# Queries, gates and merge gates as seven half-products per two column tiles, with attention run one pair of heads at a time from small buffers

## The chip, the cores and the metric

One core of one Trainium2 chip. The metric is device time in microseconds (us) of one execution of the whole program; lower is better.

## What is computed

One layer of a hybrid decoder for a prompt of 512 tokens and for 8 sampled sequences of 4 tokens each (32 tokens), so 544 tokens together. Everything starts from one projection with 18,952 columns; two branches follow, and a gated merge.

```python
u = einsum('btd,dc->btc', x, w_in)                # x: 544 x 2048; columns: q_m k_m v_m o_m z_m (2048 each),
                                                  # q_a 2048, k_a 256, v_a 256, z_a 2048, g_m g_a 2048 each, i, f
h_m, C, n, m = mlstm(q_m, k_m, v_m, i, f, state)  # 4 heads of 512; matrix memory C 512 x 512 per sequence and head
h_a = softmax(q_a k_a^T / 8 - slope * dist, sink) v_a   # 32 heads of 64, 4 key/value heads, window of 128 tokens
br_m = norm(h_m) * sigmoid(o_m) * silu(z_m);  br_a = h_a * silu(z_a)
y = sigmoid(g_m) * (br_m @ w_proj_m) + sigmoid(g_a) * (br_a @ w_proj_a)
out = layernorm(ALPHA * x + y @ w_out)
```

For the prompt a block of 128 queries sees its own block and the one before it. For the samples the queries see 128 cached keys and values and the new ones.

## The kernel before

All products are done in fp32r: each operand is split into a high part and the rest, and three of the four partial products are summed. The input is held in SBUF as such a split (a11, a21 for the first 8 of 16 row blocks k, two halves of 272 tokens each; the xk2 tiles for the other 8). A weight half (128 x 8 x 128) is loaded as `raw`, cast by ScalarE to `wh` (line 184), and VectorE subtracts to get `wl` (line 185); there are two buffers of each (`wp`).

**Plain product** (`gemm`, line 203): one column tile of 128 columns, 16 k x 3 partial products x 2 halves of 272 tokens = 96 matmuls (line 193).

**Pair** (`paired`, line 852): two column tiles as a 2 x 2 block product with 7 half-products instead of 8, each 8 k x 3 = 24 matmuls of 272 columns (lines 820 and 822), 168 in all. It needs sums of weight halves (VectorE, line 787), the seven splits, and sums of the results (`gather`, lines 831 to 850, ScalarE, GpSimd and VectorE) into two tiles O1 and O2 of the pool `ev`, which has three buffers. It needs sums of the input, too (s1, n2, n3 from `x_sums`, s4 from `last_sum`).

The order of the work:

1. Load and transpose the input; plain products for values (2 column tiles) and keys (2); the small gate product, and the gates' rows on VectorE beside them (`gates`, line 320). Split keys `ks` and values `VA` of all heads stay in SBUF.
2. For each of 16 pairs of heads k: a plain product for Q and one for Z; attention for pair k-1 runs beside them (`attn_heads`, line 507). Scores: 16 matmuls (line 525), each read by VectorE with a running maximum (line 527); Exp on ScalarE (line 538); scaling by VectorE (line 550); 8 transposes (line 559); the split of P (lines 218, 219); the own and the previous block are cut out by GpSimd products with the 0/1 masks `own_` and `prev_` (lines 564, 566); 16 matmuls of P times V (line 573); two sums (line 577) and the product with silu(z) (line 582).
3. Plain products for the first 10 of 32 merge-gate tiles; beside seven of them the sample attention (`sample_attention`, line 666) and the input sums.
4. 51 pairs: per mLSTM head six for v, k, q and four for o, z (`end_oz`, line 1071), then 11 for the other merge gates. Beside them the sample heads of the mLSTM (`sample_head`, line 1007): each loads, updates and stores 8 memories C of 1 MB from two buffers.
5. Plain products with w_proj_a beside the prompt's mLSTM; then w_proj_m; then w_out with the layer norm.

Work "beside" a product is a Python generator: `spawn` puts it on a list, and `tick` lets each take one step (to its next `yield`). `paired` calls `tick` after half-products 1, 3, 5 and 6, four times in a pair. This fixes the order in which instructions are traced; a list scheduler then places them on the engines at compile time, by that order, by dependences and by free buffers. Each engine's instructions run in the placed order. All DMAs are issued from the SP queue, in order.

Of the kernel before, what the change touches and what calls it, by code (L numbers as in the profile page):

```python
# [21 lines left out]
SEQ = 512  # L22
# [51 lines left out]
def _build(tc, nc, i, o, es):  # L74
# [59 lines left out]
    cc = cst.tile([128, C_N], F32, name="cc")  # L134
# [17 lines left out]
    esP = ExitStack()  # L152
    sp = pool(esP, "sp", 1)
    gas = sp.tile([128, 16, NS], F32, name="gas")
    qas = sp.tile([128, 2, NB, GRP, NTS], F32, name="qas")
    kas = sp.tile([128, 2, NS], F32, name="kas")
    vas = sp.tile([32, 256], F32, name="vas")

    d_brm = dr.tile([16, 128, T], F32, name="d_brm")
    d_bra = dr.tile([16, 128, T], F32, name="d_bra")  # L160
    d_q = dr.tile([16, 128, T], F32, name="d_q")
# [84 lines left out]
    esB = ExitStack()  # L246
    b1 = pool(esB, "b1", 1)
    bk = pool(esB, "bk", 4)
    esG = ExitStack()
    t544 = pool(esG, "t544", 17)  # L250
# [32 lines left out]
    nc.sync.dma_start(cc[:, 128:C_N], i["consts"][:, 128:C_N])  # L283
# [147 lines left out]


    VA = b1.tile([128, 4, KVH, 128], F32R, name="VA")
    kbp = b1.tile([128, 256], F32, name="kbp")
    vbp = b1.tile([128, 256], F32, name="vbp")
    kns = b1.tile([32, 256], F32, name="kns")
    own_ = b1.tile([128, 128], F32, name="own_")
    prev_ = b1.tile([128, 128], F32, name="prev_")
    V.tensor_scalar(own_[:], cc[:, C_TRI:C_TRI + 128], -1.0, None, op0=ALU.is_ge)
    V.tensor_scalar(prev_[:], own_[:], -1.0, 1.0, op0=ALU.mult, op1=ALU.add)  # L440
    ks = {}

    def attn_values(kk, vt):
        pt = sm()
        for b in range(4):
            PE.transpose(pt[:, b * 128:b * 128 + 128], vt[:, b * 128:b * 128 + 128], ident)
        pt2 = sm()
        PE.transpose(pt2[:32, 0:128], vt[:, SEQ:T], ident)
        src = pt[:].rearrange("p (b k d) -> p b k d", b=4, k=2)
        hilo(src, VA[:, :, 2 * kk:2 * kk + 2, 0:64], VA[:, :, 2 * kk:2 * kk + 2, 64:128])  # L450
        V.tensor_copy(vbp[:, kk * 128:kk * 128 + 128], pt[:, 384:512])
        V.tensor_copy(vas[:, kk * 128:kk * 128 + 128], pt2[:32, 0:128])
        if kk == 1:
            nc.sync.dma_start(vb_p[0].rearrange("t k d -> t (k d)"), vbp[:])
            for b in range(NB):
                nc.sync.dma_start(vb_s[b, 124:128].rearrange("t k d -> t (k d)"), vas[b * NTS:b * NTS + NTS])

    def attn_keys(kk, kt):
        for a in range(2):
            k1 = bk.tile([128, SEQ], F32R, tag="k1", name=nm("k1"))  # L460
            k2 = bk.tile([128, SEQ], F32R, tag="k2", name=nm("k2"))
            own, oth = slice(a * 64, a * 64 + 64), slice(64 - a * 64, 128 - a * 64)
            V.tensor_copy(k1[own], kt[own, 0:SEQ])
            A.copy(k1[oth], kt[own, 0:SEQ])
            V.tensor_tensor(out=k2[own], in0=kt[own, 0:SEQ], in1=r32(k1[own]), op=ALU.subtract)
            V.tensor_tensor(out=k2[oth], in0=kt[own, 0:SEQ], in1=r32(k1[own]), op=ALU.subtract)
            ks[2 * kk + a] = (k1, k2)
        yield
# [3 lines left out]
        V.tensor_copy(kbp[:, kk * 128:kk * 128 + 128], pt[:, 0:128])  # L472
        V.tensor_copy(kns[:, kk * 128:kk * 128 + 128], pt[:32, 128:256])
        if kk == 1:
            nc.sync.dma_start(kb_p[0].rearrange("t k d -> t (k d)"), kbp[:])
            for b in range(NB):
                nc.sync.dma_start(kb_s[b, 124:128].rearrange("t k d -> t (k d)"), kns[b * NTS:b * NTS + NTS])

    for kk in range(2):
        ps = gemm(win, VA_ + kk * 128, xh, xl, raws=((raw0[0], raw0[1]), (raw0[2], None))[kk])  # L480
        if kk == 0:
            spawn(gates(gates_product()))
        vt = ev()
        A.copy(two(vt[:]), pv(ps))
        attn_values(kk, vt)
    for kk in range(2):
        ps = gemm(win, KA + kk * 128, xh, xl)
        kt = ev()
        A.copy(two(kt[:]), pv(ps))
        V.tensor_copy(kas[:, kk], kt[:, SEQ:T])  # L490
        g_ = attn_keys(kk, kt)
        next(g_)
        spawn(g_)
    drain()
    esG.close()
    esB2 = ExitStack()
    b2 = pool(esB2, "b2", 2)
    bq = pool(esB2, "bq", 6)
    bs = pool(esB2, "bs", 6)
    bP = pool(esB2, "bP", 2)  # L500
    bt = pool(esB2, "bt", 1)
    bz = pool(esB2, "bz", 2)
    bm = pool(esB2, "bm", 4)
    nc.sync.dma_start(kb_s[:, 0:124], i["state_attn_k"][:, NTS:128])
    nc.sync.dma_start(vb_s[:, 0:124], i["state_attn_v"][:, NTS:128])

    def attn_heads(k, qs, hT):

        kvh = k // 4
        k1, k2 = ks[kvh]  # L510
        nb = b2.tile([128, 2, 256], F32, tag="nb", name=nm("nb"))
        for a in range(2):
            G.tensor_scalar(nb[:, a], cc[:, C_DIST:C_DIST + 256], -SLOPES[2 * k + a], None, op0=ALU.mult)
        sums = bm.tile([128, 4, 2], F32, tag="sums", name=nm("sums"))
        mx = bm.tile([128, 4, 2], F32, tag="mx", name=nm("mx"))
        mn = bm.tile([128, 4, 2], F32, tag="mn", name=nm("mn"))
        S = []
        for j in range(4):
            w0 = 128 if j == 0 else 0
            k0 = max(j - 1, 0) * 128  # L520
            pp = sm()
            s_ = bs.tile([128, 2, 256], F32, tag="s", name=nm("s"))
            for a in range(2):
                for n, kx in enumerate((k1, k2)):
                    PE.matmul(pp[:, a * 256 + w0:a * 256 + 256], qs[a][:, j * 128:j * 128 + 128],  # L525
                              kx[:, k0:k0 + 256 - w0], start=(n == 0), stop=(n == 1))
                V.tensor_tensor_reduce(s_[:, a, w0:256], pp[:, a * 256 + w0:a * 256 + 256], nb[:, a, w0:256], 1.0,  # L527
                                       sinkb[:, 2 * k + a:2 * k + a + 1], ALU.add, ALU.max,
                                       accum_out=mx[:, j, a:a + 1])
            S.append(s_)  # L530
            if j == 1:
                yield
        V.tensor_scalar(mn[:], mx[:], -1.0, None, op0=ALU.mult)
        for j in range(4):
            w0 = 128 if j == 0 else 0
            for a in range(2):
                s_ = S[j][:, a, w0:256]
                A.activation(s_, s_, AF.Exp, bias=mn[:, j, a:a + 1], accum_out=sums[:, j, a:a + 1])
# [15 lines left out]
        for a in range(2):  # L554
# [23 lines left out]
            if a == 0:  # L578
                yield
# [939 lines left out]
```

## Time and profile before

| | |
|---|---|
| three runs, median (lowest, highest) | 2608.9 us (2605.08, 2615.58) |
| the profiled execution's own time | 2608.22 us |
| its span | 2606.4 us |
| granted TensorE clock, mean | 0.996 of full |
| stage 1 (to the first Q product) | about 0 to 90 us |
| stage 2 (attention) | about 90 to 577 us |
| stage 3 (gate tiles, sample attention) | about 577 to 688 us |
| stage 4 (pairs) | 688 to 1870 us |
| stage 5 | 1870 to 2606 us |

How to read the profile: PE is TensorE (PEld its weight loads, which overlap the matmuls), DVE is VectorE, ACT ScalarE, POOL GpSimd, SP the queue that issues DMAs. "L193" is line 193 of the kernel. A row of a group gives the line, the engine, the operation, output <- inputs, the shape, how often (x), busy us and mean ns, then the engine's idle time just before these instructions and what ended it. In the chain of waits each row is a stretch of the chain that ended last: start, duration, what ran. Matmul durations are latencies of a pipeline: what one costs is the distance from one start to the next.

### The profile page before, as it was taken

Reading aid. Unit: us, or ns where it says so; the run is one execution under the profiler, and the core shown is the slowest. Engines: PE = TensorE matmul, PEld = TensorE weight load, DVE = VectorE, ACT = ScalarE, POOL = GpSimd, SP = SyncE. Lnnn points to the kernel's source line nnn. Section 1 sums busy time; section 2 is a strip of 40 time slices with the busy share of each in tenths; the row PEclk is TensorE's granted clock in tenths of the full one; section 3 lists DMA queues with packets and bytes.
Section 4 is the critical chain, followed back from the end, with each engine's and each line's share of the span. In section 5 each row is a group of like instructions: output and inputs, shape, how many; then the busy total and the mean of one; then the engine's idle time right before and its main releaser. Section 6 shows DMA issues by size and latency. Waiting matters only on the chain.

```text
span 2606.4 us, 48797 instructions
## 1 busy us (share of the span) xinstructions
PE 2572.9 (99%) x20378; PEld 2508.7 (96%) x20378; DVE 1657.6 (64%) x2428; ACT 1013.1 (39%) x1562; POOL 479.7 (18%) x467
## 2 busy tenths in 40 slices
PE   8999999999999999999999999999999999999997
PEld 8999999999999999999999999999999999999997
DVE  5666656646667877787787778777766553333336
ACT  3345545544334433433443343444633332222221
POOL 0245554541001220122122112200000000000002
PEclk9999999999999999999999999999999999999999
DMA  6322233243444575377447745764555455445432
GB/s 184 84 82 82 82 94 82 74 139 91 132 128 117 178 232 177 108 226 243 132 134 232 216 113 172 246 188 123 177 177 171 159 163 165 132 140 178 115 93 90
DMA packets 513229, 381.33 MB, mean 146 GB/s; under 512 B 30912, under 2 KB 435216, under 8 KB 512720
## 3 DMA queue, kind: packets, MB, share of 16 engines
q1 hardware_dynamic: 513008, 378.21, 48.5%
q8 instruction: 160, 2.62, 0.4%
q14 instruction: 61, 0.50, 0.1%
HBM read 295.43 MB, written 84.75 MB: 146 GB/s over the span
## 4 chain that ended last, share of the span: by engine, by line
PE 89%; DMA 6%; DVE 3%; issue 1%; ACT 1%; POOL 0%; SPq 0%; DVEq 0%; ACTq 0%; POOLq 0%
PE mm L193 41%; PE mm L820 24%; PE mm L822 11%; DMA C<-in_state_mlstm_C 3%; PE sm L1185 2%; DMA out<-C 2%; PE sm L1217 1%; PE sm L525 1%; PE sm L1030 1%; PE sm L1230 1%; PE sm L573 1%; ACT wh L184 1%; DVE wl L185 1%; PE sm L193 1%; PE sm L1034 1%
## 5 line engine op out<-in xcount | busy, mean ns | idle before, releaser
L184 ACT CAST wh<-raw 128x1024 fp32r<-128x1024 f32 x541 | 567.3, 1049 | 1123.3 <-PE mm L820 563.5
L185 DVE TENSOR_TENSOR wl<-raw,wh 128x1024 fp32r<-128x1024 f32 x541 | 702.0, 1305 | 348.6 <-ACT wh L184 345.7
L787 DVE TENSOR_TENSOR raw<-raw,raw 128x1024 f32<-128x1024 f32 x204 | 255.1, 1250 | 2.9 <-DMA raw<-in_w_in 0.2
L193 PE MATMUL mm<-xk,wh 128*128 128x272 f32 x1472 | 248.7, 290 | 0.0
L820 PE MATMUL mm<-xk,wh 128*128 128x272 f32 x1632 | 222.4, 288 | 1.1 <-ACT ev L839 1.1
L820 PEld LDWEIGHTS mm<-xk,wh 128*128 128x128 f32 x1632 | 211.8, 188 | 7.2 <-issue 3.4
L193 PE MATMUL mm<-bh,wl 128*128 128x272 f32 x1024 | 214.0, 289 | 0.0
L193 PE MATMUL mm<-bh,wh 128*128 128x272 f32 x1024 | 213.7, 290 | 0.0
L193 PE MATMUL mm<-bl,wh 128*128 128x272 f32 x1024 | 213.3, 288 | 0.0
L193 PEld LDWEIGHTS mm<-xk,wh 128*128 128x128 f32 x1472 | 208.4, 189 | 0.2
L840 POOL TENSOR_TENSOR ev<-p,ev 128x272 f32<-128x272 f32 x51 | 72.2, 1416 | 563.7 <-ACT ev L839 563.7
L193 PEld LDWEIGHTS mm<-bh,wh 128*128 128x128 f32 x1024 | 160.7, 188 | 2.3 <-issue 2.3
L193 PEld LDWEIGHTS mm<-bl,wh 128*128 128x128 f32 x1024 | 161.4, 188 | 0.0
L193 PEld LDWEIGHTS mm<-bh,wl 128*128 128x128 f32 x1024 | 160.8, 189 | 0.0
L193 PE MATMUL mm<-xk,wl 128*128 128x272 f32 x736 | 153.1, 289 | 0.0
L527 DVE CUSTOM_DVE_ANT_0 s<-sm,nb,sinkb 128x256 f32<-128x256 f32 (+1 forms) x128 | 57.2, 449 | 117.4 <-PE sm L525 117.3
L822 PE MATMUL mm<-xk,wl 128*128 128x272 f32 x816 | 118.4, 287 | 0.0
L193 PEld LDWEIGHTS mm<-xk,wl 128*128 128x128 f32 x736 | 115.8, 189 | 0.0
L820 PE MATMUL mm<-n2h,wh 128*128 128x272 f32 x408 | 107.2, 295 | 3.5 <-ACT wh L184 3.5
L193 PE MATMUL mm<-a11h,wl 128*128 128x272 f32 x368 | 108.4, 294 | 0.0
L193 PE MATMUL mm<-a11l,wh 128*128 128x272 f32 x368 | 108.3, 294 | 0.0
L822 PEld LDWEIGHTS mm<-xk,wl 128*128 128x128 f32 x816 | 108.3, 188 | 0.0
(436 smaller groups left out, 6255.1 us busy)
## 6 DMA issues: line engine op xcount, KB each, us to landing
raw<-in_w_in SPq DMA_DIRECT2D x296, 512.0 KB
C<-in_state_mlstm_C SPq DMA_DIRECT2D x32, 1024.0 KB
out<-C SPq DMA_DIRECT2D x64, 512.0 KB
raw<-in_w_proj_a SPq DMA_DIRECT2D x32, 512.0 KB
raw<-in_w_proj_m SPq DMA_DIRECT2D x32, 512.0 KB
raw<-in_w_out SPq DMA_DIRECT2D x32, 512.0 KB
d_sga<-ev SPq DMA_DIRECT2D x16, 272.0 KB
d_sgm<-ev SPq DMA_DIRECT2D x16, 272.0 KB
```

The source lines that it names most:

```text
L184: A.copy(wh[:], raw[:])
L185: V.tensor_tensor(out=wl[:], in0=raw[:], in1=r32(wh[:]), op=ALU.subtract)
L193: PE.matmul(ps[:, f, :w], a[:, kk], b(k, c, w), start=(k == 0 and n == 0), stop=(k == 15 and n == 2))
L525: PE.matmul(pp[:, a * 256 + w0:a * 256 + 256], qs[a][:, j * 128:j * 128 + 128], kx[:, k0:k0 + 256 - w0], start=(n == 0), stop=(n == 1))
L527: V.tensor_tensor_reduce(s_[:, a, w0:256], pp[:, a * 256 + w0:a * 256 + 256], nb[:, a, w0:256], 1.0, sinkb[:, 2 * k + a:2 * k + a + 1], AL ...
L573: PE.matmul(po[:, b * 128:b * 128 + n], VA[:, b, kvh], P_[:, 2 * b:2 * b + n // 128], start=(b == 0 and m == 0), stop=(b == 3 and m == 1), ...
L787: V.tensor_tensor(out=w[out][:], in0=w[a][:], in1=w[b][:], op=ALU.add)
L820: PE.matmul(ps, wh[:, k], x(p, k), start=(first and k == 0 and p == 0), stop=False, skip_group_check=True)
L822: PE.matmul(ps, wl[:, k], x(0, k), start=False, stop=(k == 7), skip_group_check=True)
L840: G.tensor_tensor(out=c22, in0=p1, in1=c11, op=ALU.subtract)
L1030: PE.matmul(pC[c * 32:c * 32 + 32, :], qz[:, c], ct[:, c], start=(b == 0), stop=(b == NB - 1), tile_position=(0, c * 32))
L1185: PE.matmul(pp[:, 0:258], a[:, b * 128:b * 128 + 128], b_[:, b, f], start=(b == 0 and n == 0), stop=(b == 3 and n == 2))
```

## The change

Q and Z of a pair of heads k become one pair (Q tile, Z tile), and each merge gate pair is (GA tile, GM tile); no gate tile is a plain product any more. There are 72 pairs: 16 for Q and Z, 40 for the mLSTM, 16 for the merge gates. Only values and keys are plain products.

To have room for the input sums during attention, attention's buffers shrink: the split keys and values of one key/value head at a time (written to DRAM as they are computed, read back and split again every fourth pair of heads), scores tiles for one pair of heads, one sz, one hT. Values are used with their differences: `DV[j] = V[j] - V[j-1]`, so that P times V is `V[j-1] P + DV[j] (own P)`; only the product with `own_` is left on GpSimd, and P times V has 14 matmuls of 128 columns per head instead of 8 (6 of 256 columns, 2 of 128). The alibi table `nb` is scaled by ScalarE. The sample columns of q, z, k, v go to DRAM and are read back by the sample attention, which runs when all heads are done. Only then are the pools of the mLSTM's sample heads opened, in the memory that attention and sample attention held; `end_oz` asks for this. `tick` is called after half-products 0, 1, 3, 4 and 6. The core of the diff:

```diff
+    s1, n2, n3 = quad(act2, "s1"), quad(act2, "n2"), quad(act2, "n3")
...
-    t544 = pool(esG, "t544", 17)
+    t544 = pool(esG, "t544", 12)
+    tx = pool(esG, "tx", 4)
...
+        nc.sync.dma_start(d_vr[0:SEQ, cs].rearrange("(b p) c -> p b c", p=128), blk(vr[:]))
...
+        nc.sync.dma_start(d_ka[kk], kt[:])
...
-    for kk in range(2):
-        ps = gemm(win, VA_ + kk * 128, xh, xl, raws=((raw0[0], raw0[1]), (raw0[2], None))[kk])
-        if kk == 0:
-            spawn(gates(gates_product()))
...
+    for kk in range(2):
+        ps = gemm(win, VA_ + kk * 128, xh, xl, raws=((raw0[0], raw0[1]), (raw0[2], None))[kk], every=4)
+        if kk == 0:
+            spawn(x_sums())
+            gates_ps = gates_product()
...
-            if n % 2 or n == 6:
+            if n in (0, 1, 3, 4, 6):
                 tick()
...
+    def open_attention():
+        for name, bufs in (("b1", 1), ("bs", 2), ("bt", 1), ("bq", 2), ("bm", 2)):
+            bp[name] = pool(esB, name, bufs)
...
+    def kv_head(kvh):
+        kk, r = kvh // 2, (kvh % 2) * 64
+        raw = scores_tile()
...
+        for half in (0, 64):
+            nc.sync.dma_start(kraw[half:half + 64], d_ka[kk, r:r + 64, 0:SEQ])
+        nc.sync.dma_start(vraw, d_vr[0:SEQ, kvh * 64:kvh * 64 + 64].rearrange("(b p) c -> p b c", p=128))
...
+        hilo(kraw, k1[:], k2[:])
+        hilo(vraw, VA[:, :, 0:64], VA[:, :, 64:128])
+        V.tensor_tensor(out=dv[:, 1:4], in0=vraw[:, 1:4], in1=vraw[:, 0:3], op=ALU.subtract)
+        hilo(dv[:, 1:4], DV[:, 1:4, 0:64], DV[:, 1:4, 64:128])
...
+    def attention(k, qs, sz, kv):
...
+        for a in range(2):
+            nb = btile("b1", [128, 256], f"nb{a}")
+            A.activation(nb[:], cc[:, C_DIST:C_DIST + 256], AF.Copy, scale=-SLOPES[2 * k + a])
...
+            st.append((s_, mx, mn, sums, sink))
+            yield
...
+            for o_, p_ in ((oh, ph), (ol, pl)):
+                G.tensor_tensor(out=o_[:], in0=r32(p_[:]), in1=own_[:].unsqueeze(1).to_broadcast([128, 4, 128]),
+                                op=ALU.mult)
+            yield
...
+            for j in range(4):
+                o_ = slice(j * 128, j * 128 + 128)
+                if j:
+                    todo += [(o_, VA[:, j - 1], p_[:, j]) for p_ in (ph, pl)]
+                todo += [(o_, DV[:, j] if j else VA[:, 0], p_[:, j]) for p_ in (oh, ol)]
+            for n, (o_, v_, p_) in enumerate(todo):
+                PE.matmul(po[:, o_], v_, p_, start=(n == 0), stop=(n == len(todo) - 1), skip_group_check=True)
...
+    def end_qz(k):
+        def end(o1, o2):
+            until(lambda: state["open"] and state["done"] == k)
...
+            nc.sync.dma_start(d_qa[k], o1[:, SEQ:T])
+            sz = btile("b1", [128, T], "sz")
+            A.activation(sz[:], o2[:], AF.Sigmoid)
+            V.tensor_tensor(out=sz[:], in0=o2[:], in1=sz[:], op=ALU.mult)
+            nc.sync.dma_start(d_bra[k][:, SEQ:T], sz[:, SEQ:T])
+            waiting[k] = (qs, sz)
...
+    def attentions():
+        while gates_ in live:
+            yield
+        for _ in last:
+            pass
+        esG.close()
+        open_attention()
+        state["open"] = True
+        for k in range(16):
+            if k % 4 == 0:
+                kv = kv_head(k // 4)
+            while k not in waiting:
+                yield
+            yield from attention(k, *waiting.pop(k), kv)
+            state["done"] = k + 1
+        esB.close()
+        yield from sample_attention()
+        esT.close()
+        open_samples()
+        state["samples"] = True
...
     def end_oz(k):
         def end(o, z_):
-            sg = pz.tile([128, T], F32, tag="sz", name=nm("sz"))
+            until(lambda: state["samples"])
+            sg = st1([128, T], "sz", p="pz")
...
+    fill = merge_gates[:8] + [w for h in range(3) for w in vkq(h)]
+    work = [fill.pop(0) for _ in range(5)]
+    n_fill = len(fill)
+    for k in range(16):
+        work.append(pair(QA + k * 128, ZA + k * 128, end_qz(k)))
+        while len(fill) > n_fill * (15 - k) // 16:
+            work.append(fill.pop(0))
+    for h in range(MH):
+        if h == 3:
+            work += vkq(h)
+        work += oz(h)
+    work += merge_gates[8:]
```

`until(cond)` calls `tick` until the condition holds. The list of pairs is then: five of merge gates; 16 of Q and Z with 21 fillers among them (the other three of the first eight gate pairs, then v, k, q of mLSTM heads 0 to 2); o, z of heads 0, 1 and 2; head 3; eight of merge gates. The last part of the constants is loaded only for the layer norm at the end.

More of the change, by code (lines that the diff above doesn't have):

```diff
@@ L458, in attn_keys @@
-    def attn_keys(kk, kt):
[L459 to L468, printed above, removed]
+        cs = slice(kk * 128, kk * 128 + 128)
@@ L486, in _build @@
[L486 to L503, printed above, removed]
```

495 lines of the change are left out of this document (229 added, 266 removed).

## The prediction

> **What bounds the kernel now.** First the page: the span, busy time by engine, the chain that ended last.
>
> ```profile
> span 2606.4 us, 48797 instructions
> PE 2572.9 (99%) x20378; PEld 2508.7 (96%) x20378; DVE 1657.6 (64%) x2428; ACT 1013.1 (39%) x1562; POOL 479.7 (18%) x467
> PE 89%; DMA 6%; DVE 3%; issue 1%; ACT 1%; POOL 0%; SPq 0%; DVEq 0%; ACTq 0%; POOLq 0%
> ```
>
> TensorE is the bound from end to end: its idle time is 33.5 us. So only two things move the time: how many matmuls there are, and whether anything newly makes TensorE wait. The windows by stage show who could.
>
> ```profile
> core 0: us, PE busy (x) PEld busy (x) DVE busy (x) ACT busy (x) POOL busy (x), PEclk, DMA share, GB/s
> 100.00:580.00 480.00, 480.00 (x3884) 480.00 (x3884) 283.76 (x593) 239.16 (x486) 239.62 (x238) 1.00 0.31 87
> 688.00:850.00 162.00, 160.72 (x1270) 158.94 (x1269) 117.63 (x124) 70.33 (x87) 15.18 (x13) 1.00 0.46 132
> 850.00:1700.00 850.00, 841.93 (x6524) 795.72 (x6523) 664.32 (x753) 344.03 (x423) 165.60 (x151) 1.00 0.61 185
> ```
>
> Row one is attention beside plain products (VectorE 59% busy), row two pairs alone (73%), row three pairs with sample heads (78%), and there TensorE still idles under 1%. The executed run took 2608.22 us for a span of 2606.4; the median of the three runs is 2608.9, so the sum is made against 2608.2 and stands 0.7 under the median.
>
> **Columns that become pairs.** The chain of waits in order of time, attention stage and pair stage (start, us, what):
>
> ```profile
> 179.42 6.04 PE mm L193 x48
> ...
> 208.11 6.00 PE mm L193 x48
> ```
>
> ```profile
> 691.72 4.29 PE mm L820 x32
> ...
> 712.13 1.06 ACT wh L184
> 713.24 4.29 PE mm L820 x32
> ```
>
> ```profile
> L193 PE MATMUL mm<-xk,wh 128*128 128x272 f32 x1472 | 248.7, 290 | 0.0
> ```
>
> 48 matmuls in 6.04 us are 0.1258 each, so a column tile of 96 takes 12.08. A pair takes 21.52 from one start to the next: 168 x 0.1258 = 21.1 and 0.4 for a cast of weights (the ACT row) that comes a little late. The last row's group runs 1472 times, 32 to a column tile (eight k, two input halves, two column halves): 46 tiles. Four stay (values, keys); 32 tiles of Q and Z and 10 of gates become 21 pairs. Removed 42 x 12.08 = 507.4, added 21 x 21.52 = 451.9: **-55.5**.
>
> **Attention's own matmuls.** The attention period, 179.42 to 208.11, is 28.7; less two column tiles, 4.5 for 40 matmuls: 16 of scores, 8 transposes, 16 of P times V. Scores and transposes stay. P times V becomes 14 matmuls per head, each 128 wide, in place of 8 (six of them 256 wide); the columns in total are equal.
>
> ```profile
> 221.29 0.60 PE L559 MATMUL sm<-cc,s 128*128 128x128 f32 x4
> ```
>
> ```profile
> 231.01 0.76 PE sm L573 x7
> ```
>
> Four 128-wide matmuls end 0.60 after the first starts, the last lasting 0.27: 0.11 from one to the next. Seven of P times V, mostly 256 wide, take 0.76: 0.11 as well. Width hardly matters, the count does: 12 more per pair of heads x 0.11 x 16 = **+21**. Bounds: 0 if columns alone counted, 12 x 0.1258 x 16 = +24. I take 21, by the row of the same width. The Trainium skill ("TensorE: Matmul & The Clock Gate", Back-to-back issue gap) puts a sustained 128-wide matmul at about 81 ns; by it this term would be an estimated +16 (12 x 0.081 x 16). The rows here show 110, and they decide.
>
> Without any new wait this gives 2608.2 - 55.5 + 21 = 2573.7. The rest is waits.
>
> **Attention beside pairs: VectorE (in order).** Groups in the attention stage, then two pair groups of the page (shape, count, busy us, mean ns, idle before):
>
> ```profile
> L185 DVE TENSOR_TENSOR wl<-raw,wh 128x1024 fp32r<-128x1024 f32 x68 | 92.4, 1359 | 17.3 <-ACT wh L184 16.9
> L527 DVE CUSTOM_DVE_ANT_0 s<-sm,nb,sinkb 128x256 f32<-128x256 f32 x96 | 46.1, 481 | 65.8 <-PE sm L525 65.7
> L550 DVE TENSOR_TENSOR s<-s,sums 128x256 f32<-128x256 f32 x64 | 26.6, 473 | 0.5
> L577 DVE TENSOR_TENSOR hT<-sm,tmp 64x512 f32<-64x512 f32 x32 | 21.9, 684 | 5.7 <-ACT tmp L576 4.0
> L219 DVE TENSOR_TENSOR pl<-sm,ph 128x512 fp32r<-128x512 f32 x32 | 21.8, 683 | 0.8 <-issue 0.3 <-ACT ph L218 0.2
> L599 DVE SCALAR_TENSOR_TENSOR q<-mm,q 64x544 fp32r<-64x544 f32 x30 | 21.7, 722 | 1.3
> L607 DVE TENSOR_TENSOR sz<-mm,sz 128x544 f32<-128x544 f32 x16 | 11.6, 725 | 2.1 <-ACT sz L606 0.5
> L527 DVE CUSTOM_DVE_ANT_0 s<-sm,nb,sinkb 128x128 f32<-128x128 f32 x32 | 11.2, 351 | 51.6 <-PE sm L525 51.6
> L527 DVE DVE_READ_ACCUMULATOR2_ANT mx<- 128x1 f32 x128 | 10.7, 83 | 0.0
> ```
>
> ```profile
> L787 DVE TENSOR_TENSOR raw<-raw,raw 128x1024 f32<-128x1024 f32 x204 | 255.1, 1250 | 2.9 <-DMA raw<-in_w_in 0.2
> L840 POOL TENSOR_TENSOR ev<-p,ev 128x272 f32<-128x272 f32 x51 | 72.2, 1416 | 563.7 <-ACT ev L839 563.7
> ```
>
> A pair costs VectorE 117.63 / 162 x 21.52 = 15.6 us (seven subtractions of L185, four sums of L787, four gathers). A pair of heads costs it: scores 6 x 0.481 + 2 x 0.351 + 8 x 0.083 = 4.3; q 1.4; z 0.7; P scaled, the same elements, 1.9; pl 1.4; hT 1.4; some 2 for small columns and a quarter of the re-split keys and values: 13.1. Between two Q,Z pairs the list puts one filler pair (11 times) or two (5). With one, TensorE has 2 x 21.52 + 52 x 0.11 = 48.8 and VectorE 2 x 15.6 + 13.1 = 44.3 (91%); with two, 70.3 and 59.9. So TensorE stays the bound on average. But 9.6 of the 13.1 (q, scores, scaling) fall into the first five of the seven half-products after a Q,Z pair: 5 x 15.6 / 7 + 9.6 = 20.7 against TensorE's 5 x 3.07 + some 2.5 = 18. The two buffers of split weights give a lead: the subtraction for half-product s+2 can start when s is over and is needed two thirds into s+2, 3.07 + 2.05 later, less its own 1.3: 3.8. An excess of 2.7 fits. What doesn't is waiting: VectorE waits for scores 65.7 + 51.6 = 117.3 us before, 7.3 per pair of heads, and what is queued behind such a wait are the subtractions TensorE needs next. Before, VectorE had nothing else to do; now the order of instructions can put subtractions there. From about 1.1 us of waiting on, each us costs TensorE one. Bounds: 0 (as in row three of the windows, 78% busy, nothing lost) and 2.7 + 7.3 - 3.8 = 6.2 x 16 = +99. I take 1.5 us of waiting, 0.4 x 16 = **+6**, near row three, since that row is this very loop with extra work.
>
> ScalarE is no bound: 70.33 / 162 x 21.52 = 9.3 per pair and, from row one, 239.16 / 480 x 28.7 = 14.3 per pair of heads, its casts for plain products still in it: at most 32.9 of 48.8. Keys and values come back from memory four times, loaded when the pair of heads before is done, two or three half-products (6 to 9 us) before the first scores that read them: 0, and up to +10 if they land late, since scores hold up TensorE's queue. GpSimd loses work (below).
>
> **Sample attention.** It now runs after the last pair of heads, and the end step of the first O,Z pair forces all of it to be issued before that pair's two `ev` tiles (of three) come free, because its `sz` tile lies in memory that sample attention holds. Before (start, us):
>
> ```profile
> 573.60 0.58 SPq L669 DMA_DIRECT2D kb<-in_state_attn_k  x1
> ```
>
> ```profile
> 621.62 1.25 DVE L708 TENSOR_REDUCE sast<-E 128x8 f32<-128x1056 f32 x1
> ...
> 630.72 0.29 DVE L718 TENSOR_SCALAR E<-E,sast 128x128 f32<-128x128 f32 x1
> ```
>
> ```profile
> 670.33 2.41 DVE L744 TENSOR_TENSOR gas<-sm,gas 64x128 f32<-64x128 f32 x8 [1.62 <-PE sm L738]
> ```
>
> There it was spread over 97 us of plain products. Its softmax alone is a chain of 9.4 (621.62 to 631.0); around it four rounds of keys and four of values, an estimated 2.5 each from operations of 0.2 to 0.6 us like those on lines 682 to 738, 20; with 3.5 for the O,Z step 33, and 38 if the loads land 5 us after the pair's end. Meanwhile TensorE has five of the next pair's seven half-products, 15.4, and an estimated 9 of the sample attention itself: some 10 uncovered. Bounds 0 (the chain starts early) and +30 (loads land late, no cover). **+10**.
>
> **The rest.** The sample heads get five turns per pair instead of four and end with the last pair: 32 loads and as many stores of 1 MB (C) pass in 26 pairs instead of some 36. TensorE waited little for C before (us, times, longest), and the first branch loads were issued at 1709.5:
>
> ```profile
> PE sm L1030 <- DMA C<-in_state_mlstm_C: 6.1, 9, 1.1
> ```
>
> ```profile
> L1058 SPq DMA_DIRECT2D pf<-d_bra x11: 319/430/574, 1709.5 to 1717.1; - x11
> ```
>
> Twice that wait at most doubles it, and those branch loads, 160 us ahead of the stage that starts at about 1870, are now issued in the last pair: **+2**, bounds 0 and +15. Input sums move beside the key and value products, the gate rows beside the first five pairs, where no attention is open yet; VectorE has 5.9 us free per pair; TensorE hides both: **+1** (bounds 0 and +5; without that cover the sums' 28 operations on 128x544, 0.72 each by row L607, would show as up to 20). Fewer input buffers, the constants in two loads, d_qa and gate stores on SP: a few issues of some 0.5 us (the kb row) beside weight loads with a lead of two half-products: 0; 3 if SP stalls behind one.
>
> Sum: -55.5 + 21 + 6 + 10 + 2 + 1 = -15.5: **2593**.
>
> **Rivals.** *No new wait*: 2574, spoken for by row three of the windows. *VectorE takes over*: the waits for scores stay at half, 3.65 per pair of heads: 2.7 + 3.65 - 3.8 = 2.5 x 16 = +41 in place of +6, **2628**, slower. It decides from 1.1 us on; the 117.3 speaks for it, row three against. *Sample attention uncovered* and the tail late: +30 and +9 for +10 and +2, **2620**: no change. *GpSimd blocks VectorE*:
>
> ```profile
> 208.07 2.27 DVE L185 TENSOR_TENSOR wl<-raw,wh 128x1024 fp32r<-128x1024 f32 x1 [0.18 <-ACT wh L184]
> ```
>
> ```profile
> 209.23 2.26 POOL L564 TENSOR_TENSOR Ph<-ph,own__341 128x512 fp32r<-128x512 f32 x1
> ```
>
> The subtraction took 0.9 us longer than its mean while the two overlapped. But with GpSimd busy 50% of that stage a subtraction took 1359 on the mean against 1250 for the sums of the pairs, 109 x 68 = 7 us of 239.6: rare.
>
> ```profile
> L566 POOL TENSOR_TENSOR Pl<-pl,prev__342 128x384 fp32r<-128x384 f32 x32 | 32.5, 1014 | 0.0
> L566 POOL TENSOR_TENSOR Ph<-ph,prev__342 128x384 fp32r<-128x384 f32 x32 | 32.4, 1012 | 0.0
> L513 POOL TENSOR_SCALAR nb<-cc 128x256 f32<-128x256 f32 x28 | 23.8, 852 | 2.5 <-DVE mx L527 0.8
> ```
>
> These three leave GpSimd: 14.3 per pair of heads becomes 8.8, and each pair brings 1.42. If all of it held VectorE up, 44.3 would be 44.3 + 8.8 + 2.8 = 55.9, 7.1 over TensorE, x 11, and with two fillers 59.9 + 13.1 - 70.3 = 2.7 x 5: 92 in place of 6, **2679**. The Trainium skill says it so ("SBUF — State Buffer", SBUF: two separate sides): the shared port pair is an exclusive lock and the loser "fully blocks". The one pair of rows agrees, the means show that it seldom comes to that.
>
> **Chances.** Forecast 0.46 (2581 to 2605), no new wait 0.15, VectorE takes over 0.22, sample attention uncovered 0.14, GpSimd 0.03. About 0.5% (13 us) can be told from no change. Faster: 0.15 and two thirds of 0.46, some 0.47; same: 0.15 and most of 0.14, 0.27; slower 0.26. Range 2571 to 2636: it leaves out GpSimd and the upper third of the VectorE case.
>
> **What would show it.** Right: plain L193 products with xk down to 128 calls, 72 pairs, pair period 21.5 between Q,Z pairs, P times V at 0.11; VectorE near 90% in the attention stage and TensorE idle there under 10 us; one gap of about 10 us after the first O,Z pair. Wrong: TensorE waiting for L185 over and over in the attention stage (VectorE case), a gap of 30, subtractions near 2 us on the mean (GpSimd), or TensorE waiting for C.

## The result and the profile after

| | us, median (lowest, highest) |
|---|---|
| before, beside it | 2608.2 (2605.08, 2615.58) |
| after | 2668.4 (2666.34, 2671.46) |
| ratio | 1.0227, 95% interval 1.0204 to 1.0251: slower |

The profiled execution of after took 2671.46 us. Its page has span, busy time, and the slices of TensorE and its granted clock:

```profile
span 2669.2 us, 48843 instructions
PE 2573.3 (96%) x20066; PEld 2491.3 (93%) x20066; DVE 1868.2 (70%) x2626; ACT 1123.0 (42%) x1746; POOL 456.9 (17%) x360
...
PE   8999999999999999989999999999999999999997
...
PEclk9999999999999999997999999999999999999999
```

TensorE ran 312 instructions fewer than before, 504 gone (42 column tiles x 96 less 21 pairs x 168) and 192 added, just as the prediction counted, and yet its busy time is about that of before, 2573.3 us against 2572.9. Expected was 2572.9 - 55.5 + 21 = 2538.4, so 34.9 us of busy time are more than the count of the matmuls explains. The mean granted clock fits that: 0.983 against 0.996, which by itself is an estimated 35 us (0.017 of 2669.2 less 0.004 of 2606.4). TensorE's idle time is 2669.2 - 2573.3 = 95.9 us against 33.5, 62.4 more. Together 97.3: nearly all of the distance from the sum without new waits, 2573.7, to 2671.5, which is 97.8. TensorE waited, and part of the time it ran slowly.

Where it waited is read from the waits of TensorE (what it waited for, us in all, times, longest), first in attention (160 to 1166 us), then around the sample attention (1166 to 1245), then beside the sample heads (1245 to 1933):

```profile
PE mm L572 <- ACT ev L596: 14.8, 16, 0.9
PE sm L719 <- POOL ol L707: 13.0, 3, 4.3
PE mm L572 <- ACT wh L181: 12.6, 37, 0.6
```

```profile
PE sm L853 <- DVE E L845: 7.8, 1, 7.8
PE mm L572 <- DVE ev L594: 3.8, 1, 3.8
PE mm L572 <- ACT wh L181: 2.2, 1, 2.2
```

```profile
PE sm L1030 <- DMA C<-in_state_mlstm_C: 12.0, 10, 3.2
```

In attention three rows of different engines make up the 40.4 us of idle time. One wait comes once per pair of heads (16), one only at the three switches of the key/value head. To see what each costs, look at the first low-part matmul of successive pairs in the timeline (start, duration):

```profile
425.55 1.25 PE L574 MATMUL mm<-a11h,wl 128*128 128x272 f32 x8
...
457.39 1.17 PE L574 MATMUL mm<-a11h,wl 128*128 128x272 f32 x8
...
478.91 0.92 PE L574 MATMUL mm<-a11h,wl 128*128 128x272 f32 x6
...
504.21 1.13 PE L574 MATMUL mm<-a11h,wl 128*128 128x272 f32 x7
...
529.70 1.17 PE L574 MATMUL mm<-a11h,wl 128*128 128x272 f32 x8
...
1166.12 1.17 PE L574 MATMUL mm<-a11h,wl 128*128 128x272 f32 x8
...
1238.02 1.25 PE L574 MATMUL mm<-a11h,wl 128*128 128x272 f32 x8
```

A pair with a head of attention beside it takes 25.3 or 25.5 us, 50.8 for the two (478.91 to 529.70) where 48.8 was the sum: 2.0 x 16, some 33 us (the **steady loss**). The pair at a switch (425.55) takes 31.8, 6.5 more than its neighbours, three times: 20 us (the **switches**). The pair that the sample attention falls into takes 71.9 (1166.12 to 1238.02), 50.4 over 21.5. Before, sample attention took some 25 from the same TensorE: of the 113 us from 577 to 690, 228 calls of this group, at 32 to a column tile, are 7.1 tiles or 86 us, 14 calls of the first pair are 1.8, and 25 are left.

```profile
L193 PE MATMUL mm<-xk,wh 128*128 128x272 f32 x228 | 39.4, 295 | 0.0
```

So 25 us are lost there (the **hold**). The second pair takes 28.5, 7 too many, but 2 of them are 19 matmuls for the gates' rows, which before had elsewhere. The four plain products end at 87.5 us, in before at 80.5 with the same matmuls. That makes some 12 us (the **start**). What is left of the 97.8, some 8, falls to the pairs beside the sample heads, where the waits for C alone grew by 5.9. The windows show the clock's part: all of attention, a switch (425.6), one ordinary pair of heads (478.9), the hold, and two stretches beside the sample heads, each right after one of the two longest waits for C (2.9 and 3.2 us):

```profile
core 0: us, PE busy (x) PEld busy (x) DVE busy (x) ACT busy (x) POOL busy (x), PEclk, DMA share, GB/s
160.00:1166.00 1006.00, 965.64 (x7568) 950.38 (x7567) 815.70 (x1108) 527.07 (x883) 241.08 (x153) 0.99 0.37 104
425.60:478.90 53.30, 48.80 (x367) 48.12 (x366) 38.15 (x43) 23.27 (x30) 11.70 (x6) 0.94 0.36 101
478.90:529.70 50.80, 49.07 (x390) 48.23 (x389) 43.38 (x63) 28.04 (x50) 13.87 (x9) 1.00 0.35 101
1190.00:1226.00 36.00, 29.37 (x153) 22.48 (x154) 8.59 (x36) 5.88 (x20) 2.36 (x4) 0.50 0.06 12
1537.10:1540.50 3.40, 3.40 (x18) 2.33 (x11) 0.00 (x0) 0.00 (x0) 0.40 (x2) 0.50 0.90 258
1861.40:1868.10 6.70, 6.04 (x25) 4.28 (x26) 0.75 (x1) 0.00 (x0) 1.97 (x3) 0.50 0.87 307
```

Over attention VectorE is busy 81% of the time, in a full period 85%: high, not full. The 36 us of the hold from 1190 on, with the end of the wait of 7.8 us for the softmax, have a clock of 0.50.

What happens at a switch, in order of time:

```profile
434.18 4.97 POOL L707 TENSOR_TENSOR ol<-pl,own__1500 128x512 fp32r<-128x512 f32 x1 [1.83 <-DVE pl L216]
...
434.55 1.21 DVE L539 TENSOR_TENSOR raw<-raw,raw 128x1024 f32<-128x1024 f32 x1
...
435.69 2.34 DVE L182 TENSOR_TENSOR wl<-raw,wh 128x1024 fp32r<-128x1024 f32 x2
437.96 0.42 DVE L594 SCALAR_TENSOR_TENSOR ev<-mm,p 128x272 f32<-128x272 f32 x1
...
439.21 0.47 PE L719 MATMUL sm<-ol,VA 128*128 128x128 f32 x1 [4.33 <-POOL ol L707]
```

GpSimd's product ol takes 4.97 us; the same work on oh takes 1.41 where little runs beside it:

```profile
508.70 1.41 POOL L707 TENSOR_TENSOR oh<-ph,own__1500 128x512 fp32r<-128x512 f32 x1 [3.09 <-ACT ph L215]
```

VectorE has no gap at that moment, since the splits of the new keys and values have pushed weight work behind them. In these rows GpSimd makes no end as long as VectorE runs operations with two inputs in SBUF back to back (L539, L182); it ends 1.2 us after VectorE has reached one that reads PSUM (L594). P times V waits for ol, and the next half-products are queued behind it. The clock falls before the wait is over, and stays at half for 6.8 us:

```profile
438.00:444.80 6.80, 5.59 (x25) 5.59 (x26) 1.85 (x5) 1.34 (x3) 3.02 (x3) 0.50 0.72 193
```

And what happens once in every pair of heads, on ScalarE:

```profile
491.63 1.28 ACT L690 ACT_TABLE_LOAD   x1
...
492.93 0.40 ACT L690 ACTIVATE s<-s,mn 128x128 f32<-128x128 f32 x1
...
494.81 0.28 ACT L693 ACTIVATE mx<-mn,sinkb 128x4 f32<-128x4 f32 x1
...
494.99 0.38 ACT L596 ACTIVATE ev<-mm 128x272 f32<-128x272 f32 x1
...
495.42 0.39 PE L572 MATMUL mm<-s4h,wh 128*128 128x272 f32 x1 [0.93 <-ACT ev L596]
```

The exponentials of a head need another activation table than the sigmoid in sz. The load and nine short instructions stand ahead of gather's copy out of PSUM (L596), and the next half-product into that tile waits 0.93 us for it.

**Theory:** TensorE waits for single late instructions. Each is late because of what stands ahead of it in its queue, or because two engines hold each other up; and the clock adds to it. **Rival:** VectorE is full in attention (the prediction's "VectorE takes over"), so only the amount of its work counts. All runs below stand against after at 2668.4; before, run again beside each group of them, stayed between 2608.3 and 2609.8.

### The profile page after: what moved, and what is told of

Read it like the earlier page. It is cut to its first block, busy times and chain, and to the rows that moved or that the text cites. A ratio compares the mean times of both kernels' runs of the same rounds, so it can differ in the third digit from the quotient of the medians.

```text
span 2669.2 us, 48843 instructions
## 1 busy us (share of the span) xinstructions
PE 2573.3 (96%) x20066; PEld 2491.3 (93%) x20066; DVE 1868.2 (70%) x2626; ACT 1123.0 (42%) x1746; POOL 456.9 (17%) x360
## 4 chain that ended last, share of the span: by engine, by line
PE 72%; DVE 9%; ACT 7%; DMA 5%; issue 2%; POOL 1%; SPq 0%; ACTq 0%; DVEq 0%; POOLq 0%
PE mm L572 27%; PE mm L190 20%; PE mm L574 12%; DVE raw L539 3%; DMA C<-in_state_mlstm_C 3%; DVE wl L182 3%; ACT wh L181 2%; ACT s L690 2%; DMA out<-C 2%; PE sm L1203 2%; PE sm L1235 1%; PE sm L679 1%; PE sm L1030 1%; PE sm L719 1%; PE sm L1248 1%
## 5 line engine op out<-in xcount | busy, mean ns | idle before, releaser
L182 DVE TENSOR_TENSOR wl<-raw,wh 128x1024 fp32r<-128x1024 f32 x604 | 808.7, 1347 | 322.1 <-ACT wh L181 303.3
L539 DVE TENSOR_TENSOR raw<-raw,raw 128x1024 f32<-128x1024 f32 x288 | 361.1, 1258 | 3.2 <-DMA raw<-in_w_in 0.8
L572 PE MATMUL mm<-xk,wh 128*128 128x272 f32 x2304 | 318.4, 291 | 0.0
L572 PEld LDWEIGHTS mm<-xk,wh 128*128 128x128 f32 x2304 | 302.2, 191 | 2.5 <-issue 0.8
L190 PE MATMUL mm<-bh,wl 128*128 128x272 f32 x1024 | 214.8, 289 | 0.0
L592 POOL TENSOR_TENSOR ev<-p,ev 128x272 f32<-128x272 f32 x72 | 104.5, 1452 | 642.5 <-ACT ev L591 642.5
L190 PE MATMUL mm<-bh,wh 128*128 128x272 f32 x1024 | 214.2, 289 | 0.0
L190 PE MATMUL mm<-bl,wh 128*128 128x272 f32 x1024 | 212.8, 288 | 0.0
L572 PE MATMUL mm<-s4h,wh 128*128 128x272 f32 x576 | 150.0, 292 | 14.8 <-ACT ev L596 14.8
L190 PEld LDWEIGHTS mm<-bh,wh 128*128 128x128 f32 x1024 | 160.9, 188 | 1.5 <-issue 1.5
L190 PEld LDWEIGHTS mm<-bl,wh 128*128 128x128 f32 x1024 | 161.2, 188 | 0.8 <-DVE bl L216 0.8
L190 PEld LDWEIGHTS mm<-bh,wl 128*128 128x128 f32 x1024 | 161.0, 189 | 0.0
L572 PE MATMUL mm<-n3h,wh 128*128 128x272 f32 x576 | 149.8, 292 | 3.8 <-DVE ev L594 3.8
L572 PE MATMUL mm<-s1h,wh 128*128 128x272 f32 x576 | 150.3, 291 | 2.0 <-ACT p L583 2.0
L572 PE MATMUL mm<-s1l,wh 128*128 128x272 f32 x576 | 150.0, 291 | 0.0
L572 PE MATMUL mm<-n3l,wh 128*128 128x272 f32 x576 | 149.9, 291 | 0.0
L572 PE MATMUL mm<-n2l,wh 128*128 128x272 f32 x576 | 149.6, 291 | 0.0
```

Of the source, the lines that this page charges most:

```text
L182: V.tensor_tensor(out=wl[:], in0=raw[:], in1=r32(wh[:]), op=ALU.subtract)
L190: PE.matmul(ps[:, f, :w], a[:, kk], b(k, c, w), start=(k == 0 and n == 0), stop=(k == 15 and n == 2))
L539: V.tensor_tensor(out=w[out][:], in0=w[a][:], in1=w[b][:], op=ALU.add)
L572: PE.matmul(ps, wh[:, k], x(p, k), start=(first and k == 0 and p == 0), stop=False, skip_group_check=True)
L592: G.tensor_tensor(out=c22, in0=p1, in1=c11, op=ALU.subtract)
```

## Experiments: one loss at a time

**Six pairs ahead of the hold.**

```diff
-        while len(fill) > n_fill * (15 - k) // 16:
+        while len(fill) > (20 - k if k < 15 else 0):
```

> One filler pair after each of the first 15 Q,Z pairs and six after the last, so that about six pairs stand between the last Q,Z pair and the hold for the sample attention. Theory (the 50.4 us that the pair after the hold takes over its 21.5 are some 24 us of TensorE work and the rest waits, 14 us of them in the trace, and the half clock that follows them): that pair falls to about 21.5 and the sample attention spreads over the others, 2640 us (2634 to 2648). Rival (the sample attention costs TensorE the same wherever it stands, or the hold only moves): 2663 to 2670.

Measured: 2646.9, 21.5 less. The pairs around the sample attention lose their waits (7.8, 3.8) altogether, but one pair still takes 47.4 and another 28.2, 32.6 over two plain pairs and not the 25 of before. The windows show why:

```profile
1087.30:1104.00 16.70, 16.52 (x131) 15.80 (x130) 13.70 (x32) 10.08 (x28) 1.67 (x3) 1.00 0.51 139
1104.00:1134.60 30.60, 30.60 (x184) 26.30 (x184) 10.91 (x22) 3.42 (x7) 0.00 (x0) 0.67 0.06 22
```

From 1104 on TensorE is never idle, and the granted clock falls to 0.67: much of that stretch is 128 matmuls of 32 columns each (P times V of the samples). So it was not the wait alone that brought the clock down. Before shows it more plainly. From 634.7 to 638.3 TensorE ran thirty of these narrow matmuls there, nothing between them and no idle time; from 637.8 on the clock was at half:

```profile
637.90:641.20 3.30, 3.30 (x17) 3.12 (x16) 0.28 (x1) 0.27 (x1) 0.00 (x0) 0.50 0.43 127
```

**No switch.**

```diff
-            if k % 4 == 0:
-                kv = kv_head(k // 4)
+            if k == 0:
+                kv = kv_head(0)
```

> Keys and values of the first key/value head are used for all heads, so that nothing is read back and split at pairs of heads 4, 8 and 12 (this leaves out that part of the computation). Theory (at each switch the extra splits make GpSimd's own product late, TensorE waits 4.3 us and then runs at half clock; 6.5 us each): the three gaps of 32 us fall to 25.4, 2649 us (2645 to 2653). Rival (VectorE is full and only its work counts, 2.6 us of splits per switch): 2660 us.

Measured: 2649.3, 19.1 less; the three gaps are 25.3 to 25.5. The switches cost what the ledger said, 20, not the 8 of the rival.

**More work for VectorE.**

```diff
+            for _ in range(2):
+                V.tensor_tensor(out=hT[:], in0=cc[:, 0:512], in1=cc[:, 0:512], op=ALU.add)
             V.tensor_tensor(out=sums[:], in0=sums[:], in1=mx[:], op=ALU.add)
```

> Four additions of 128x512 that nobody needs are put on VectorE in every attention, 0.68 us each, 2.7 us per pair of heads. Theory (VectorE, busy 43.4 of 50.8 us, isn't full; TensorE waits for single late instructions): the period stays within 0.6 us of 50.8, 2668 to 2678 us. Rival (VectorE is the bound of attention): 16 times 2.7 us more, 2711 us.

Measured: 2671.3, 2.9 more. The rival's 43 are not there: **VectorE is not the bound**. But the 2.9 is a balance. By the starts of the pairs, the 13 pairs of heads without a switch took 0.9 us more each on the mean, where at most 0.6 was expected, with a wait that after has only twice (2.0 us):

```profile
PE mm L572 <- ACT p L583: 17.6, 24, 1.5
```

The three switches took 10 us less together: the waits for ol fell from 13.0 to 4.7 us, one long one in place of three, since the added work had changed the order of the instructions. So a third of the added time does show. Not all of that need be VectorE's load: the added sums write hT, and six of them waited for its store, 11.1 us in all.

**No table load before the softmax.**

```diff
-            A.activation(sz[:], o2[:], AF.Sigmoid)
+            A.activation(sz[:], o2[:], AF.Exp)
```

> The sigmoid in sz becomes an exponential (so sz is z exp(z) and not silu(z)), and ScalarE needs no table load between sz and the softmax. Theory (each Q,Z pair waits 0.9 us for the copy of gather at L596, which stands behind a table load of 1.28 us and the exponentials on ScalarE): that wait goes 16 times, 2653 us (2650 to 2658). Rival (VectorE full, ScalarE doesn't matter): 2666 to 2670 us.

Measured: 2646.1, 22.3 less. The 25.3 of every pair of heads became 24.1, and the waits for L596 are gone from TensorE's list: 1.2 x 16 = 19, more than the wait of 0.93 itself. What the rest is stays open.

**The product ol on VectorE.**

```diff
-                G.tensor_tensor(out=o_[:], in0=r32(p_[:]), in1=own_[:].unsqueeze(1)...
+                (V if p_ is pl else G).tensor_tensor(out=o_[:], in0=r32(p_[:]), in1=own_[:].unsqueeze(1)...
```

> The product of the low part of P with the mask (ol) is made by VectorE and not by GpSimd; all else as after. Theory (GpSimd's product stands still while VectorE runs operations on SBUF back to back, and takes 4.97 us at the three switches): the three waits of 4.3 us for ol go with the half clock behind them, 2650 us (2647 to 2656), at a price on VectorE that the run with the added load puts at 3 us or less. Rival (at a switch the splits make everything late, whoever multiplies): 2665 to 2671.

Measured: 2631.3, 37.1 less, twice what was expected. The switches are at 25.3, as expected; but every second pair of a pair of heads also fell from 25.5 to 24.4. The page of this kernel, the group of L707 on VectorE, and the waits for casts:

```profile
PE 2557.6 (97%) x20066; PEld 2481.3 (94%) x20066; DVE 1867.1 (71%) x2658; ACT 1122.8 (43%) x1746; POOL 406.1 (15%) x328
```

```profile
L707 DVE TENSOR_TENSOR ol<-pl,own__1500 128x512 fp32r<-128x512 f32 x32 | 29.3, 917 | 0.0
```

```profile
PE mm L572 <- ACT wh L181: 5.4, 26, 0.3
```

VectorE got 32 operations of 29.3 us more and is busy 1867.1 us, where after had 1868.2. So GpSimd's product must have kept VectorE waiting for about as long as VectorE takes to do it itself. After has it in the timeline, the casts' sums (two of L539) beside ol; e5's follow below it:

```profile
503.46 2.14 POOL L707 TENSOR_TENSOR ol<-pl,own__1500 128x512 fp32r<-128x512 f32 x1 [1.83 <-DVE pl L216]
...
504.73 3.10 DVE L539 TENSOR_TENSOR raw<-raw,raw 128x1024 f32<-128x1024 f32 x2
```

```profile
495.10 0.67 DVE L707 TENSOR_TENSOR ol<-pl,own__1500 128x512 fp32r<-128x512 f32 x1
495.70 2.34 DVE L539 TENSOR_TENSOR raw<-raw,raw 128x1024 f32<-128x1024 f32 x2
```

Two sums take 3.10 beside GpSimd and 2.34 without, and the casts behind them are late by that. In after a half-product then waits 0.57 for such a cast (at 507.9, one of the 37 waits for casts in after's list), once per pair of heads; in e5 that wait is gone. The Trainium skill ("SBUF — State Buffer", SBUF: two separate sides) says of the shared port pair that whichever starts first holds it for the whole instruction, also a VectorE operation with two SBUF inputs against a GpSimd one that reads SBUF. Both directions are in these rows: 3.10 for 2.34 on VectorE, 4.97 for 1.41 on GpSimd.

**Later splits.**

```diff
+        scores_tile()
         raw = scores_tile()
```

> The raw keys and values take the other of the two scores buffers, which comes free only when the second head of the pair has been transposed; so the splits at a switch stand behind the softmax and the own products of the attention before. Theory (the splits beside the own product are what makes it late): gaps at the switches 25 to 27 us, 2649 us (2647 to 2655). Rival (any place of the splits holds TensorE up, the scores of the next pair of heads now wait for them): 2668 to 2685.

Measured: 2672.1, and ol at the first switch again takes 4.98 us, at 433.87. The list scheduler placed the splits where they had been; the edit didn't do what it was to do, and the run tells nothing about their place.

**P times V in 8 matmuls.**

```diff
-                    todo += [(o_, VA[:, j - 1], p_[:, j]) for p_ in (ph, pl)]
-                todo += [(o_, DV[:, j] if j else VA[:, 0], p_[:, j]) for p_ in (oh, ol)]
+                V.tensor_tensor(out=P_[:, 2::2], in0=r32(P_[:, 2::2]), in1=r32(P_[:, 3::2]), op=ALU.subtract)
...
+                    mv = P_[:, 2 * b + 1:2 * b + 3] if b < 3 else P_[:, 7]
```

> P times V again as 8 matmuls per head (6 of 256 columns, 2 of 128): the previous block's part is P minus its own part, subtracted by VectorE in place; no differences of values. Theory (TensorE bounds, 192 matmuls of 128 columns at 0.11 us are the 21 us that the sum set against the gain, and VectorE has room for 2 us more per pair of heads): 2649 us (2645 to 2656). Rival (two more steps between the transposes and P times V make TensorE wait longer there than the matmuls took): 2668 us or more.

Measured: 2678.4, 10 more. Page and waits:

```profile
PE 2552.1 (95%) x19874; PEld 2466.3 (92%) x19874; DVE 1909.5 (71%) x2682; ACT 1123.1 (42%) x1742; POOL 472.9 (18%) x360
```

```profile
PE mm L572 <- ACT wh L181: 24.4, 30, 2.2
PE sm L714 <- DVE Ph L707: 17.3, 16, 1.5
PE mm L572 <- DVE ev L594: 17.0, 17, 3.8
```

192 matmuls fewer take 2573.3 - 2552.1 = 21.2 us off TensorE: **the +21 of the prediction**. That it fits to the digit is chance, since the granted clock differs a little (0.985 here, 0.983 in after); but the rate holds. In after's timeline twelve of them start from 505.82 to 507.05, 0.112 apart, 21.5 for 192. And it is lost again: VectorE's subtraction must wait for GpSimd's product in the middle of the chain, and 17.3 and 13.2 us of new waits for it and for the gather behind it appear. The rival held.

**Two losses without changing the result.** The six late pairs, and

```diff
-        work.append(pair(QA + k * 128, ZA + k * 128, end_qz(k)))
+        work.append(pair(QA + k * 128, ZA + k * 128, end_qz(k), 0.5))
...
-            A.activation(sz[:], o2[:], AF.Sigmoid)
-            V.tensor_tensor(out=sz[:], in0=o2[:], in1=sz[:], op=ALU.mult)
+            A.activation(sz[:], o2[:], AF.Tanh)
+            V.scalar_tensor_tensor(sz[:], sz[:], 1.0, o2[:], op0=ALU.add, op1=ALU.mult)
```

with 0.25 for 0.125 in the three scales of Q.

> The six late fillers of the first experiment, and silu(z) as z/2 (1 + tanh(z/2)), with the factor 1/2 in the pair's scale, so that sz needs the same activation table as the softmax and the result stays that of the reference. Theory (the two losses are separate): 21.5 and 22 us off, 2625 us (2621 to 2630). Rival (they share waits, or tanh needs a table of its own): 2638 us or more.

Measured: 2629.9, 38.5 less (21.5 and 17.0). Tanh shares the table of the exponentials: of the waits for L596, 3.7 us of 14.8 are left, in the first four pairs of heads, where the sigmoids of a gate pair still force a table load.

## Experiments: the losses together, and the two small terms

**All three**: late pairs, tanh, ol on VectorE.

> The three working edits together: six late fillers, silu by tanh, ol on VectorE. Theory (three separate losses of 21.5, 17 and 37 us, of 97.8 that the change lost against a sum without new waits): 2594 us (2588 to 2602), under the kernel before. Rival (the losses overlap; with one wait gone the next engine is late): 2605 us or more.

Measured: 2594.1, ratio to before 0.9948 (0.9936 to 0.9961). 74.3 less than after, against 21.5 + 17.0 + 37.1 = 75.6 for the three alone: the losses are separate. An ordinary pair of heads now takes 24.1 + 24.4 = 48.5: with the table load and GpSimd's product out of the way, the steady loss over the 48.8 of the sum is gone.

**oh on VectorE too** (the `G.` of L707 becomes `V.`):

> As the three together, and the other own product (oh) on VectorE too, so that GpSimd has only the sum of P, the product with sz and the c22 of gather in attention. Theory (a GpSimd product keeps VectorE from SBUF for about as long as VectorE would take for it itself): within 4 us of the three together. Rival (VectorE is full by now): 16 times 1.4 us more, 2610 us or more.

Measured: 2595.0, the same. The page again has VectorE less busy with 32 operations more than its forerunner's 1868.4:

```profile
PE 2544.9 (98%) x20066; PEld 2474.3 (95%) x20066; DVE 1852.7 (71%) x2690; ACT 1089.7 (42%) x1718; POOL 369.5 (14%) x296
```

**c22 on VectorE** (the `G.` of L592 becomes `V.`):

> As the three together, and gather's c22 of every pair on VectorE, not on GpSimd. Theory (GpSimd's 1.5 us there stretches a VectorE operation beside it, but no wait of TensorE ends on it): within 4 us of the three together. If such stretching is behind the casts that come late (wh): 5 to 10 us less.

Measured: 2598.3, 4.2 more, at the edge of what was expected; no loss lies there.

**Order of the fillers and finer steps.**

```diff
-    fill = merge_gates[:8] + [w for h in range(3) for w in vkq(h)]
+    fill = [w for h in range(3) for w in vkq(h)] + merge_gates[:8]
...
-                yield
-            PT = PTs[b % 2]
+            yield
+            PT = PTs[b % 2]
```

> As the three together, with the mLSTM pairs ahead of the eight gate pairs among the fillers (so that no sigmoid stands among the exponentials of the gates' rows at the start, nor in attention), and with one step of the sample attention's P times V per sequence and not per two. Theory (the second pair loses 7 us to three table loads; thinly filled stretches of TensorE of 3 to 4 us bring the clock down): 7 and 5 us less, 2582 us (2576 to 2590). Rival (the start waits for the gates' rows in any case, the clock falls just the same): the same as the three together.

Measured: 2590.8, ratio to before 0.9936 (0.9922 to 0.9950): the fastest here, but 3.3 us less than the three, not 12. The second pair fell from 28.5 to 24.2; the pair with the sample attention only from 46.9 to 45.1. Its page has TensorE's work near what the prediction had counted (2538.4):

```profile
PE 2542.6 (98%) x20066; PEld 2473.7 (96%) x20066; DVE 1867.2 (72%) x2658; ACT 1086.9 (42%) x1716; POOL 398.3 (15%) x328
```

**The order alone**, on after:

> As after, but with the mLSTM pairs ahead of the gate pairs among the fillers; nothing else. Theory (three of ScalarE's table loads, between the gate pairs' sigmoids and the exponentials of the gates' rows, make the second pair 7 us late): the second pair falls from 28.5 to about 24 us, 2663 us (2660 to 2668). Rival (the order makes no difference without the tanh): 2666 to 2672.

Measured: 2668.7, no difference. The second pair is at 24.2 as the theory said, 4.3 us saved, and the three table loads there (at 109.5, 111.4 and 113.9 us in after) are gone. The waits for C, 14.9 us for 12.0, took most of it back. The table loads explain that pair, and the total doesn't show it. (In the runs that leave this part alone the pair takes 27.0 to 28.7, so the saving is 2.8 at the least.)

**Four turns per pair from the first O,Z pair on.**

```diff
-            if n in (0, 1, 3, 4, 6):
+            if n in ((0, 1, 3, 4, 6) if p <= 42 else (1, 3, 5, 6)):
```

> As after, but from the first O,Z pair on, the work beside the pairs gets four turns per pair (after half-products 1, 3, 5, 6), as before the change, and not five. Theory (the five turns put more transfers of C beside a pair, and TensorE waits 12.0 us for C in place of 6.1): the waits for C fall to about 6 us, and what of the sample heads is left passes beside the products with w_proj_a, 2660 us (2654 to 2666). Rival (the waits for C come from something else, or the rest of the sample heads costs later what is saved): 2666 to 2680.

Measured: 2718.8, 50.4 more: the expectation was far off. The waits for C in the whole run; the waits from 1900 us on, beside the products with w_proj_a; the window there:

```profile
PE sm L1030 <- DMA C<-in_state_mlstm_C: 23.1, 9, 10.1
```

```profile
PE sm L1030 <- DMA C<-in_state_mlstm_C: 20.2, 5, 10.1
PE sm L1034 <- POOL Ab L1021: 11.6, 6, 2.9
```

```profile
1933.00:2050.00 117.00, 94.94 (x621) 79.29 (x622) 59.57 (x128) 35.40 (x64) 8.50 (x14) 0.79 0.53 165
```

Of 23.1 us of waits for C, 20.2 lie there, so while the pairs ran they were 2.9: the denser turns are behind the 12.0. But what is left of the last sample head then meets TensorE without cover, and the clock falls again (0.79). The five turns of the change are the better choice.

## Why the prediction was wrong

The forecast was 2593, a little faster than before; measured is 2668.4, slower. The TensorE side was right: 504 matmuls gone, 192 added, some 21 us for the latter. It was also right that only waits could make the change slower, and three of the places were named (sample attention, start, sample heads). The sizes were not right: forecast 19 us, measured 97.8.

- **Attention beside pairs, +6; measured some 33.** This is the step that failed. It looked for a wait of VectorE for scores, judged the other engines by their share ("ScalarE is no bound ... at most 32.9 of 48.8"; GpSimd "seldom comes to that", from means), and put the rival at 2628 on VectorE being full. VectorE was at 85%, below the forecast 91%, and 2.7 us more of it per pair of heads cost 0.9. What was late were single instructions: a PSUM copy behind a table load on ScalarE (17 to 22 us by two runs) and VectorE's sums beside GpSimd's product (some 17); without both the period is 48.5, the forecast sum. The means of before hid this, because plain products need little of either engine in time; a pair needs a gather or a weight sum every 3 us.
- **Re-split keys and values, 0, at most +10; measured 20.** Not the landing of the data was late, as the step feared, but the splits on VectorE kept GpSimd's product from ending. The rival on the port named the right pair of engines with the wrong victim: TensorE waited for GpSimd.
- **Sample attention, +10 with bounds 0 and +30; measured some 25.** The waits were about as long as forecast (7.8 and 3.8 us for the 10); the half clock for 36 us wasn't in the sum. Six pairs in front take back 21.5.
- **Start, +1; measured some 12.** Three table loads between sigmoids and exponentials at the gates' rows are 4.3 of it, and were not counted. Nor were a wait of 2.5 us for ScalarE (L437) and two of 2.2 together for split weights (L190) ahead of the pairs, with 6.8 us at half clock (42.0 to 48.9): the four plain products end 7 us later than before.
- **Sample heads, +2 with bounds 0 and +15; measured some 8.** Waits for C doubled, as the bound had it (6.1 to 12.0), and 10 us at half clock came with them, about 5 lost.
- **The clock, not a term at all; measured 34.9,** which lie within the sizes above. Each wait was priced at its length.

Not settled: whether a later place of the splits alone would free the switches, and how much of the half clock in the hold is due to the wait and how much to the narrow matmuls.

## What to carry to other kernels

Busy shares say which engine could be the bound, not whether a product will find its next operand in time: where TensorE needs a result every 3 us, follow each queue in order and look for long or odd instructions (table loads, GpSimd products) that come to stand ahead of it. Price a TensorE wait at more than its length where it is long enough to bring the clock down (here the three waits of 4.3 us came with 6.8 us at half clock each, the sixteen of 0.93 us with none). Before moving elementwise work to GpSimd, check in the timeline what VectorE does beside it; in this kernel the two mask products were free on VectorE, the c22 of the gather was not (4.2 us more).

## What the runs showed of the hardware

- GpSimd's 128x512 product took 1.41 us where little ran beside it, 2.14 beside mixed VectorE work and 4.97 beside VectorE operations without a gap. Given back to VectorE, ol took 0.67 to 1.27 (mean 0.92) and left VectorE's total busy time the same (1867.1 against 1868.2); with oh there too it was lower (1852.7 against 1868.4).
- A wait of 4.3 us came with 6.8 us at a granted clock of 0.50, from 1.2 us before its end on; waits of 2.9 and 3.2 us were followed by 3.4 and 6.7 us at 0.50. Without any wait, 30 us with 128 matmuls of 32 columns ran at 0.67 on the mean, and thirty such matmuls in a row, 3.6 us, were followed by 0.50. The Trainium skill ("TensorE: Matmul & The Clock Gate", Part 1: The HAM clock gate) sets the clock by how busy TensorE has been; in those 30 us it was busy by the profile all the time, so matmuls that narrow may count as less than busy. No run here changed their width, so this is not shown.
- An activation table load took 1.28 us, and tanh and the exponential needed none between them.
